# Issuing five of six early input loads from the kernel's body, after VectorE's first memset, in an attention-score kernel

## The chip, the cores and the metric

The kernel runs on one core of a Trainium2 chip. The metric is the device time of one execution in microseconds (us). The kernel before the change was run three times: 201.30, 201.58 and 201.77 us, median 201.58 us. One more execution was taken with the hardware profiler; it took 201.45 us, of which the profile covers a span of 200.1 us. All times "at" some point below are counted from the start of that span.

## The reference

For each of 8 batches and 8 heads, the scores of 512 queries against 512 keys of 64 elements are computed and scaled. There is no softmax and no mask.

```python
batch, heads, seq, dim = 8, 8, 512, 64      # q and k: float32
scale = 1.0 / np.sqrt(q.shape[-1])
return (np.einsum('bhqd,bhkd->bhqk', q, k) * scale).astype(np.float32)
```

The inputs are 8.39 MB each, 16.78 MB together. The output is 8 x 8 x 512 x 512 float32, 67.11 MB. So four fifths of all bytes moved are stores.

## The kernel before

The kernel is written with one instruction stream for each engine and explicit semaphores. SyncE issues every DMA. The input is cut into four units of two batches (`UNITS = 4`), and each unit has one load of keys and one of queries, 2.1 MB each. That makes eight loads. The output goes out in 16 stores of 4.2 MB (`ALL = 16`).

The four steps of the data are these. GpSimd casts a landed load to bf16. TensorE transposes it, and VectorE and ScalarE move the transposed tiles to `kT` and `qz`. TensorE multiplies. VectorE and ScalarE scale the scores into one of three large buffers, which SyncE then stores.

The first six loads stand inside a critical section of the tile framework. It is closed and compiled before the streams of the engines begin; at its end stands a barrier of all five engines. The last two loads reuse buffers, and wait in SyncE's stream until GpSimd has cast the third and the fourth load.

```python
    def load(v, x):
        nc.sync.dma_start(out=xf(v)[:, x],
                          in_=(k_r, q_r)[x][v].rearrange("p (s c) -> p s c", s=2)
                          ).then_inc(load_sems[2 * v + x], 16)

    with tc.tile_critical(no_gpsimd_drain=True):
        for v in range(UNITS - 1):
            for x in range(2):
                load(v, x)
    tc.close()
    tc.compile()


    for x in range(2):
        nc.sync.wait_ge(sem["ready"], 3 + x)
        load(UNITS - 1, x)
    for g in range(ALL):
        nc.sync.wait_ge(sem["act"], 4 * g + 4)
        nc.sync.wait_ge(sem["dve"], 4 * g + 4)
        nc.sync.dma_start(out=out_r[g], in_=store_buffer(g).rearrange("p x i k -> p x (i k)")
                          ).then_inc(store_sems[g % 3], 16)
    # ... (waits for the last stores)
```

GpSimd's stream: it builds the identity matrix and then casts each load in two halves as it lands.

```python
    # ... (identity)
    for v in range(UNITS):
        for x in range(2):
            # ...
            nc.gpsimd.wait_ge(load_sems[2 * v + x], 16)
            # ...
            for s in range(2):
                # ... (source and destination patterns)
                cast = nc.gpsimd.tensor_copy(out=dst, in_=src)
            cast.then_inc(sem["ready"], 1)
```

VectorE's stream begins with two memsets that clear the padded query tiles; each of them raises `zeroed` by one.

```python
    def evacuator(engine, copy, scaled, parity, done, freed):
        if parity:
            for v in range(2):
                engine.memset(qz[:, v * N:(v + 1) * N], 0.0).then_inc(sem["zeroed"], 1)
        for c in range(CHUNKS):
            engine.wait_ge(sem["turn"], c + 1)
            if c == 2:
                engine.wait_ge(sem["zeroed"], 2)
            move(copy, c, parity, first[c])
        # ... (scaling the scores, moving later chunks)
```

TensorE waits, before the first scores of output blocks 0, 1 and 2, until 2, 6 and 8 loads have been cast, since the store buffers of those blocks are also load buffers. From block 3 on it waits for the store that used the buffer before.

```python
            if p == 0 and w == 1:
                if g < 3:
                    pe.wait_ge(sem["ready"], (2, 6, 8)[g])
                else:
                    pe.wait_ge(store_sems[g % 3], g // 3 * 16)
```

Of the kernel before, what the change touches and what calls it, by code (L numbers as in the profile page):

```python
# [5 lines left out]
def kernel(  # L6
# [5 lines left out]
    nc = tc.nc  # L12
# [3 lines left out]
    UNITS = B // 2  # L16
# [21 lines left out]
    sem = {name: nc.alloc_semaphore(name) for name in names}  # L38
# [31 lines left out]
    def xf(v):  # L70
        return bigs[(0, 1, 2, 1)[v]].rearrange("p x i k -> p (x i k)").rearrange(
            "p (x s c) -> p x s c", x=2, s=2)
# [4 lines left out]
# [3 lines that stand above are left out]
                          ).then_inc(load_sems[2 * v + x], 16)  # L80

    with tc.tile_critical(no_gpsimd_drain=True):  # L82
        for v in range(UNITS - 1):
            for x in range(2):
                load(v, x)
    tc.close()
    tc.compile()  # L87


    for x in range(2):  # L90
        nc.sync.wait_ge(sem["ready"], 3 + x)
        load(UNITS - 1, x)
# [152 lines left out]
```

## Time and profile before

| quantity | value |
|---|---|
| time, median of three runs | 201.58 us |
| span of the profile | 200.1 us |
| TensorE busy with matmuls | 99.9 us, 50% |
| VectorE busy | 106.1 us, 53% |
| ScalarE busy | 84.9 us, 42% |
| GpSimd busy | 39.5 us, 20%, all of it in the first quarter |
| bytes moved by DMA | 83.95 MB, mean 419 GB/s |
| mean granted TensorE clock | 0.811 of full speed |

The profile page gives the busy time of each engine, and cuts the span into 40 slices whose digits are the busy share in tenths. The chain of waits walks back from the last instruction to what released each step. The timeline lists instructions in order of time, with the idle time ahead of them and what ended it. "SPq L78" is SyncE's queue working on line 78 of the kernel, where a load is issued. The time of such an issue is not the time of the transfer: that begins about a microsecond later and ends when the semaphore of the load has reached its full count, which the profile calls the landing.

### The profile page before, as it was taken

How to read it: one execution, taken by the hardware profiler on the slowest of the kernel's cores; microseconds unless marked ns; L12 is line 12 of the kernel's file. 1: busy time of each engine (PE TensorE's matmuls, PEld its weight loads, DVE VectorE, ACT ScalarE, POOL GpSimd, SP SyncE). 2: the span in 40 equal slices, each digit the busy share in tenths (PEclk: the TensorE clock that was granted, in tenths of full speed). 3: DMA queues.
4: the chain of work that ended last, by engine and by line, in shares of the span. 5: the costliest groups of instructions: out<-in, count | busy, mean ns of one | idle time of the engine just before them, and what ended most of it. 6: DMA issues, size and time to landing. Idle time of an engine off the chain costs nothing.

```text
span 200.1 us, 1081 instructions
## 1 busy us (share of the span) xinstructions
PE 99.9 (50%) x377; PEld 47.4 (24%) x384; DVE 106.1 (53%) x98; ACT 84.9 (42%) x97; POOL 39.5 (20%) x22
## 2 busy tenths in 40 slices
PE   0027660376875757654764487365747373830000
PEld 0026430143331414312431233041202020200000
DVE  0665692076895847691769276829364544450000
ACT  0204670264693646562665266446444343430000
POOL 0399999996000000000000000000000000000000
PEclk9999997579797888995799579969696968585555
DMA  6999999999999999999999999999999999999996
GB/s 190 439 422 429 426 442 429 422 409 426 432 436 432 422 432 432 432 429 429 432 429 432 426 439 432 432 422 439 432 429 419 426 442 429 429 419 436 429 436 259
DMA packets 5509, 83.95 MB, mean 419 GB/s; under 512 B 384, under 2 KB 384, under 8 KB 384
## 3 DMA queue, kind: packets, MB, share of 16 engines
q1 hardware_dynamic: 5504, 83.89, 98.6%
q8 instruction: 3, 0.05, 0.1%
q14 instruction: 2, 0.02, 0.0%
HBM read 16.78 MB, written 67.11 MB: 419 GB/s over the span
## 4 chain that ended last, share of the span: by engine, by line
DMA 58%; DVE 12%; PE 10%; POOL 7%; issue 1%; SPq 0%
DMA out_dram<-big 42%; DVE big L212 10%; DMA big<-in_k_dram 8%; DMA big<-in_q_dram 7%; POOL xb L122 7%; PE ps L145 7%; PE tp L130 3%; DVE qz L184 2%; DVE kT L184 1%; SPq L78 0%; SPq L95 0%; SPq L87 0%; SPq L82 0%
## 5 line engine op out<-in xcount | busy, mean ns | idle before, releaser
L145 PE MATMUL ps<-kT,qz 128*128 128x512 bf16 x249 | 79.7, 454 | 61.9 <-DMA out_dram<-big 31.1
L212 DVE TENSOR_SCALAR big<-ps 128x1024 f32<-128x1024 f32 x64 | 76.9, 1222 | 52.3 <-PE ps L145 47.9
L209 ACT ACTIVATE big<-ps 128x1024 f32<-128x1024 f32 x64 | 65.0, 1024 | 71.2 <-PE ps L145 65.9
L145 PEld LDWEIGHTS ps<-kT,qz 128*128 128x128 bf16 x256 | 25.2, 110 | 109.6 <-DMA out_dram<-big 34.4
L122 POOL CAST xb<-big 128x2048 bf16<-128x2048 f32 x16 | 38.8, 2463 | 3.7 <-DMA big<-in_k_dram 3.0
L130 PE MATMUL tp<-identity,xb 128*128 128x128 f32 x104 | 19.2, 347 | 13.7 <-POOL xb L122 13.7
L130 PEld LDWEIGHTS tp<-identity,xb 128*128 128x128 f32 x104 | 17.5, 187 | 17.6 <-issue 16.5
L184 DVE COPY kT<-tp 64x512 f32<-64x512 f32 x14 | 9.7, 694 | 6.9 <-PE tp L130 6.5
L184 ACT COPY kT<-tp 64x512 f32<-64x512 f32 x14 | 8.1, 577 | 11.5 <-PE tp L130 11.1
L189 DVE MEMSET qz<- 128x4096 uint32 x2 | 6.9, 3472 | 6.7 <-PEq L87 5.9
L184 DVE COPY qz<-tp 64x512 f32<-64x512 f32 x12 | 8.3, 695 | 3.8 <-PE tp L130 3.4
L184 ACT COPY qz<-tp 64x512 f32<-64x512 f32 x12 | 7.5, 621 | 1.7 <-PE tp L130 1.6
L130 PE MATMUL ps<-identity,xb 128*128 128x128 f32 x24 | 5.6, 420 | 1.2 <-POOL xb L122 1.2
L130 PEld LDWEIGHTS ps<-identity,xb 128*128 128x128 f32 x24 | 5.0, 226 | 1.6 <-POOL xb L122 1.6
L184 DVE COPY qz<-ps 64x512 f32<-64x512 f32 x4 | 2.8, 694 | 2.1 <-PE ps L130 2.0
L184 ACT COPY qz<-ps 64x512 f32<-64x512 f32 x4 | 2.5, 625 | 2.4 <-PE ps L130 2.4
L184 ACT ACT_TABLE_LOAD x1 | 1.3, 1283 | 5.0 <-PEq L87 5.0
L184 DVE COPY kT<-ps 64x512 f32<-64x512 f32 x2 | 1.4, 694 | 0.3 <-PE ps L130 0.3
L184 ACT COPY kT<-ps 64x512 f32<-64x512 f32 x2 | 1.2, 578 | 0.6 <-PE ps L130 0.5
L102 POOL MEMSET identity<- 128x128 f32 x1 | 0.2, 205 | 4.6 <-POOLq L87 4.6
L104 POOL TENSOR_SCALAR_AFFINE_SELECT identity<-identity 128x128 f32<-128x128 f32 x1 | 0.3, 292 | 0.2 <-POOL identity L102 0.2
L229 POOL MEMSET const-float32-0.0<- 128x1 f32 x1 | 0.1, 98 | 0.2 <-issue 0.2
(3 smaller groups left out, 0.3 us busy)
## 6 DMA issues: line engine op xcount, KB each, us to landing
out_dram<-big SPq DMA_DIRECT2D x16, 4096.0 KB, 21.3
big<-in_k_dram SPq DMA_DIRECT2D x4, 2048.0 KB, 15.6
big<-in_q_dram SPq DMA_DIRECT2D x4, 2048.0 KB, 18.0
```

The costliest lines, as they stand in the source:

```text
L102: nc.gpsimd.memset(identity, 0.0).then_inc(sem["ident"], 1)
L104: nc.gpsimd.affine_select(out=identity, in_=identity, compare_op=mybir.AluOpType.not_equal, fill=1.0, base=0, pattern=[[-1, P]], channel_m ...
L122: cast = nc.gpsimd.tensor_copy(out=dst, in_=src)
L130: ins = pe.transpose(out=dst[:, w], identity=identity, in_=xw[:, c % SLOTS * W + w])
L145: ins = pe.matmul(out=pss[pair % 3][:, w, :], lhsT=qz[:, n, i + w], rhs=keys[:, n], start=True, stop=True)
L184: copy(out=dst, in_=src[:, h]).then_inc(sem["moved"], 1)
L189: engine.memset(qz[:, v * N:(v + 1) * N], 0.0).then_inc(sem["zeroed"], 1)
L209: lambda o, ps: nc.scalar.mul(out=o, in_=ps, mul=scale),
L212: lambda o, ps: nc.vector.tensor_scalar(out=o, in0=ps, scalar1=scale, scalar2=None, op0=mult),
L229: nc = _bacc.Bacc("TRN2", target_bir_lowering=False, num_devices=1)
```

## The change

All loads but the first leave the critical section. They are issued in SyncE's own stream, after a wait for VectorE's first memset. The loads keep their order, their sizes, their buffers and their semaphores, and nothing else in the kernel is touched. The purpose is to hand the first load to the DMA engines alone, and let the other five follow when the engines have come to work.

```diff
     with tc.tile_critical(no_gpsimd_drain=True):
-        for v in range(UNITS - 1):
-            for x in range(2):
-                load(v, x)
+        load(0, 0)
     tc.close()
     tc.compile()
 
 
+    nc.sync.wait_ge(sem["zeroed"], 1)
+    for n in range(1, 2 * (UNITS - 1)):
+        load(n // 2, n % 2)
     for x in range(2):
         nc.sync.wait_ge(sem["ready"], 3 + x)
         load(UNITS - 1, x)
```

## The prediction

> **What bounds the kernel now.** I read the page first: the slices, the queues, and the chain that ended last. No compute engine is busy for more than 53% of the span; the DMA engines are.
>
> ```profile
> span 200.1 us, 1081 instructions
> DMA  6999999999999999999999999999999999999996
> GB/s 190 439 422 429 426 442 429 422 409 426 432 436 432 422 432 432 432 429 429 432 429 432 426 439 432 432 422 439 432 429 419 426 442 429 429 419 436 429 436 259
> q1 hardware_dynamic: 5504, 83.89, 98.6%
> ```
>
> The DMA row is 9 in every slice but the first and the last, at a nearly constant 430 GB/s; the one queue that SyncE feeds fills 98.6% of the 16 engines' span. 83.89 MB at 430 GB/s is 195.1 us. The other 5 us of the span are the start before data flow at full rate, and the end. So **the time is the moment at which the DMA engines begin, plus 195 us, plus every hole in their work**. That is why the first ten microseconds, the only ones the change touches, matter at all.
>
> Does the work behind the loads leave holes later? The chain of waits, in order of time, shows how the stores live:
>
> ```profile
> 62.91 19.99 DMA out_dram<-big
> ...
> 90.23 22.02 DMA out_dram<-big
> ```
>
> The columns are start, length and what it was. A store of 4.19 MB needs 9.75 us at 430 GB/s, but lands 20.0 to 22.0 us after its issue, so about 12 us of older stores stand ahead of it. A buffer returned at 62.91 + 19.99 = 82.90 is full again at 90.2, after 7.3 us. The compute side could thus be several microseconds later and the DMA engines would not notice. Conversely, making it earlier buys nothing.
>
> Now the start, in the timeline (start, length, engine, line, what; in brackets the idle time before it and what ended it):
>
> ```profile
> 0.95 0.39 SPq L78 DMA_DIRECT2D big<-in_k_dram  x1
> 1.39 0.42 SPq L78 DMA_DIRECT2D big<-in_q_dram  x1
> ...
> 3.53 0.46 SPq L78 DMA_DIRECT2D big<-in_q_dram  x1
> 5.00 0.20 POOL L102 MEMSET identity<- 128x128 f32 x1 [4.56 <-POOLq L87]
> 5.00 1.28 ACT L184 ACT_TABLE_LOAD   x1 [5.00 <-PEq L87]
> ...
> 5.93 3.47 DVE L189 MEMSET qz<- 128x4096 uint32 x1 [5.93 <-PEq L87]
> 8.71 34.24 POOL L122 CAST xb<-big 128x2048 bf16<-128x2048 f32 x14 [2.98 <-DMA big<-in_k_dram]
> ```
>
> SyncE issues six loads back to back from 0.95 to 3.99, about 0.5 us each. And **GpSimd, ScalarE and VectorE all stand idle until 5.0 us or later, released by line 87**, the end of the framework's section. What line 87 waits for is seen in the view of lines 82 and 87 (count, duration in ns, first and last start):
>
> ```profile
> L82 SPq EVENT_SEMAPHORE  x1: 17/17/17, 4.0 to 4.0; - x1
> L87 SPq DRAIN  x3: 7/7/7, 4.3 to 4.6; - x3
> L87 POOLq EVENT_SEMAPHORE  x4: 17/17/17, 4.4 to 4.9; - x4
> ```
>
> SyncE reaches the barrier only after its last issue: issues done at 3.99, its section's semaphore at 4.0, the barrier's exchanges from 4.3 to 4.9, the first work at 5.0. Every engine begins late because SyncE has issued six loads first. The chip runs that barrier 1.0 us after SyncE's last issue.
>
> Last, how fast loads go. The landing times of the key loads, then of the query loads:
>
> ```profile
> DMA to landing us min/median/max: 7.7/15.6/25.2
> DMA to landing us min/median/max: 12.2/18.0/29.6
> ```
>
> And the rates by stretch (from:to, length, busy time of the five engine rows, clock, DMA share, GB/s):
>
> ```profile
> 2.00:4.00 2.00, 0.00 (x0) 0.00 (x0) 0.00 (x0) 0.00 (x0) 0.00 (x0) 1.00 1.01 246
> 4.00:6.00 2.00, 0.00 (x0) 0.00 (x0) 0.07 (x1) 1.00 (x1) 0.50 (x2) 1.00 0.94 401
> 6.00:8.00 2.00, 0.00 (x0) 0.00 (x0) 2.00 (x1) 0.29 (x1) 0.00 (x0) 1.00 0.99 426
> ```
>
> The shortest landing of each is the first of its kind: load 0 lands at 0.95 + 7.7 = 8.65, load 1 at 1.39 + 12.2 = 13.59. One load behind another costs 4.9 us (2.10 MB at 430 GB/s); a load into an idle queue costs 7.7 us, that is 2.8 us more, for the way to the first byte, the slow first packets (246 GB/s from 2 to 4 us) and the completion.
>
> **What the Trainium skill says.** "DMA: Bandwidth & Descriptors", section "Queues, rings and completion order", says that each DMA engine consumes the descriptors of one ring in order. The trace agrees: loads issued within 3 us land 4.9 us apart, in order, so load 0 already has the engines to itself. The same page, "Anatomy of one DMA", says that DMA engines wait on no semaphore; the sequencer that issues does. So the new wait stops SyncE, and only an empty ring stops the data. That section also fits a transfer (issued from GpSimd there) as about 2.0 us plus bytes at 436 GB/s, an estimate of 6.8 us for one load; the trace shows 7.7 for the first one, and the trace is used here. The section "Specifications" gives a ceiling of 435 GB/s; at the measured 430 there is about 1% left to win.
>
> **The change part by part.**
>
> *It removes* five issues from ahead of the barrier. They ran from 1.39 to 3.99. SyncE is then done at 0.95 + 0.39 = 1.34, so the barrier and everything released by it come 3.99 - 1.34 = **2.65 us earlier**: GpSimd's and ScalarE's first work at 5.00 - 2.65 = 2.35, the first memset at 5.93 - 2.65 = 3.28.
>
> *It adds* a wait for that memset's end. Its length is 3.47 us in the timeline; it ends at 5.93 + 3.47 = 9.40 before, and at 3.28 + 3.47 = **6.75** after. A wait of SyncE on a semaphore is followed by its issue within some 0.02 us elsewhere in this trace (the cast that releases the load at 23.41 ends at 23.39). Load 1 is therefore issued at 6.77 instead of 1.39.
>
> *It moves* loads 1 to 5. Load 0 still lands at 8.65. The question is whether the rings run dry between load 0 and load 1. Bytes moved by 8.0 us, from the stretches (25, 246, 401 and 426 GB/s for 2 us each) are 2.20 MB, and load 0 is 2.10 MB, so its last bytes pass at about 7.8 on average. Load 1's first bytes come about 1.0 us after its issue, as those of load 0 did (issue 0.95, flow just before 2.0): at about 7.8. **The two meet within a few tenths of a microsecond.** Two limits bracket the cost:
> - rings never dry: load 1 lands 4.9 us after load 0, at 13.55, as before. Cost 0.
> - rings dry, with the whole start-up paid again: load 1 lands at 6.77 + 7.7 = 14.47 instead of 13.59. Cost 0.9 us.
>
> I choose 0.4: a ring that is just running empty will likely lose a part of the slow start.
>
> *What it reaches.* GpSimd casts a load in 2 x 2.45 = 4.9 us, exactly the DMA's pace, so it can't catch up: a load that lands 0.4 later is cast 0.4 later, and the last two loads, issued on the third and fourth cast (23.41 and 28.31), go out at about 23.8 and 28.7. Load 5 lands at 33.5, so the queue holds work all along. The first store, issued at 31.18 before, also has loads ahead of it. So no further hole opens, and the 0.4 arrives at the end undiminished. The 2.65 us won by VectorE, ScalarE and GpSimd are worth nothing, since the first cast waits for load 0, which lands when it did.
>
> Sum: 201.58 + 0.4 = **202.0 us**.
>
> **The rivals.**
>
> *The barrier doesn't move* (something other than SyncE's issues holds the engines to 5 us). Then load 1 goes out at 9.42, the rings are dry from 7.8, and load 1 lands at 9.42 + 7.7 = 17.1, 3.5 us late: 205.1 us, still 1.8%. For it speaks that VectorE's memset starts 0.9 us after ScalarE's first work, so a part of its delay is its own; but the second memset also starts 0.80 us after the first with nothing to wait for, so that part seems to belong to the memset, and moves along. Against it speaks the order of events at lines 82 and 87.
>
> *The first load gains from being alone* and lands sooner than 8.65, so that casting begins sooner. The slow first packets lie in the time in which SyncE issues the other five, which speaks for it; but the rings serve in order, and then GpSimd only waits for load 1. The end is set by load 1's flow, so time stays at 201.6 to 202.5.
>
> *Compute becomes the bound*, because casts and first scores shift. The 12 us of queued stores speak against it: a shift below that is hidden.
>
> *A gain*: the earlier engine start shortens the kernel. It needs a start of the data flow before 2 us, which nothing in the change moves, so at most a few tenths.
>
> **Range and chances.** The bracket is 201.6 to 202.5, the three runs spread by 0.5, and the start-up could cost a little more when GpSimd's and VectorE's work lies beside it: 201.3 to 203.0. Two per cent is 4.0 us; even the barrier rival stays inside. Chances: faster 0.01, within 2% 0.97, slower 0.02.
>
> **What would show each step.** The profile after should have the first memset at about 3.3 us, SyncE's second issue at about 6.8, load 0 landing near 8.6, load 1 at 13.5 to 14.5, later landings 4.9 us apart, a dip in the rate between 7 and 9 us, and 430 GB/s from then on. The prediction is wrong if the memset still begins at 5.9, if the rate dips for over 1 us, or if a later slice falls below 9.

## The result and the profile after

The changed kernel takes 202.45 us, the median of four runs (202.25 to 202.50), against 201.46 us for the kernel before on the same chip (201.30 to 201.77). That is 0.99 us more; the ratio is 1.0046, with a 95% interval of 1.0028 to 1.0063. So it is slower by half a per cent, a difference far below 2% but clear of noise.

The page of the changed kernel first, the same rows as were shown before:

```profile
span 201.2 us, 1081 instructions
DMA  6999999999999999999999999999999999999995
GB/s 205 345 433 420 433 443 423 420 388 437 427 430 430 433 432 425 433 433 433 420 440 423 433 430 437 430 423 440 427 433 420 433 443 423 430 427 430 433 437 254
q1 hardware_dynamic: 5504, 83.89, 98.6%
```

The DMA row still reads 9 from the second slice on, so at this resolution nothing has changed. The row below it tells where the time went: the second slice (5 to 10 us) moved 345 GB/s where it had moved 439. Over 5.03 us, 94 GB/s less is 0.47 MB, or 1.1 us at 430 GB/s. The first slice moved slightly more than before (205 against 190, worth 0.2 us). The slice that starts at 40 us moved 388 where it had moved 409; every other slice between the first two and the last lies within 12 GB/s of before.

The timeline of the start (start, length, engine, line, what; in brackets the idle time before and what ended it):

```profile
0.95 0.39 SPq L78 DMA_DIRECT2D big<-in_k_dram  x1
2.34 0.20 POOL L103 MEMSET identity<- 128x128 f32 x1 [1.90 <-POOLq L85]
2.34 1.28 ACT L185 ACT_TABLE_LOAD   x1 [2.34 <-PEq L85]
...
3.27 3.47 DVE L190 MEMSET qz<- 128x4096 uint32 x1 [3.27 <-PEq L85]
6.77 0.34 SPq L78 DMA_DIRECT2D big<-in_q_dram  x1
...
8.75 4.81 POOL L123 CAST xb<-big 128x2048 bf16<-128x2048 f32 x2 [5.68 <-DMA big<-in_k_dram]
...
14.63 9.75 POOL L123 CAST xb<-big 128x2048 bf16<-128x2048 f32 x4 [1.08 <-DMA big<-in_q_dram]
```

The engines are released 2.66 us earlier, the memset begins at 3.27 instead of 5.93, and load 1 is issued at 6.77. The first cast begins at 8.75, almost as before (8.71): load 0 landed at 8.69 against 8.66, so having the DMA engines to itself brought it nothing. The new item is the last line: GpSimd, which used to cast 14 halves without a pause, now waits 1.08 us for load 1.

The view of lines 82 and 85, the end of the critical section (count, duration in ns, first and last start):

```profile
L82 SPq EVENT_SEMAPHORE  x1: 17/17/17, 1.4 to 1.4; - x1
...
L85 POOLq EVENT_SEMAPHORE  x4: 17/17/17, 1.7 to 2.2; - x4
```

SyncE reaches the barrier at 1.4 instead of 4.0, and the barrier follows at the same distance. Then the shortest landings of the key loads and of the query loads, and below them the rates by stretch (the last figure is GB/s, the one before it the DMA share; a packet counts whole in the stretch in which it begins, so a share can exceed 1):

```profile
DMA to landing us min/median/max: 7.7/13.5/21.2
DMA to landing us min/median/max: 7.8/15.9/25.5
```

```profile
6.00:8.00 2.00, 0.00 (x0) 0.00 (x0) 1.20 (x2) 0.00 (x0) 0.00 (x0) 1.00 1.26 442
8.00:10.00 2.00, 0.00 (x0) 0.00 (x0) 2.00 (x1) 0.00 (x0) 1.25 (x1) 1.00 0.75 229
10.00:12.00 2.00, 0.00 (x0) 0.00 (x0) 1.01 (x1) 0.00 (x0) 2.00 (x2) 1.00 1.03 442
```

Load 0 takes 7.7 us and load 1 takes 7.8, from issue to landing: load 1 pays the start-up of an idle queue nearly whole, and lands at 14.58 instead of 13.55. From 8 to 10 us the rate is 229 GB/s. The later landings, read from the semaphores in the trace, are 19.48, 24.38, 29.27 and 34.16, so 4.9 us apart and each 1.02 to 1.03 us later than before. The last DMA write ends at 200.72 instead of 199.68, 1.04 us later. **A hole of 1 us at 9 us runs through to the end undiminished.**

The chain of waits shows that the stores still have a queue ahead of them:

```profile
91.41 21.89 DMA out_dram<-big
...
148.34 23.60 DMA out_dram<-big
```

At 9.75 us for one store's bytes, 22 to 24 us from issue to landing means 12 to 14 us of older stores in front. Compute never became the bound.

### The profile page after: what moved, and what is told of

The parts are those of the page before. It is cut to its first block, busy times and chain, and to the rows that moved or that the text cites. A ratio compares the mean times of both kernels' runs of the same rounds, so it can differ in the third digit from the quotient of the medians.

```text
span 201.2 us, 1081 instructions
## 1 busy us (share of the span) xinstructions
PE 98.3 (49%) x377; PEld 46.8 (23%) x384; DVE 106.1 (53%) x98; ACT 84.7 (42%) x97; POOL 39.4 (20%) x22
## 4 chain that ended last, share of the span: by engine, by line
DMA 56%; DVE 14%; PE 9%; POOL 7%; issue 1%; ACT 1%; SPq 0%
DMA out_dram<-big 42%; DVE big L213 9%; DMA big<-in_q_dram 7%; POOL xb L123 7%; DMA big<-in_k_dram 6%; PE ps L146 6%; PE tp L131 3%; DVE qz L185 2%; DVE qz L190 2%; DVE kT L185 1%; ACT big L210 1%; SPq L78 0%; SPq L96 0%
## 5 line engine op out<-in xcount | busy, mean ns | idle before, releaser
L146 PE MATMUL ps<-kT,qz 128*128 128x512 bf16 x249 | 78.1, 443 | 63.0 <-DMA out_dram<-big 32.2
L146 PEld LDWEIGHTS ps<-kT,qz 128*128 128x128 bf16 x256 | 24.6, 109 | 109.7 <-DMA out_dram<-big 35.4
```

The source lines that it names most:

```text
L146: ins = pe.matmul(out=pss[pair % 3][:, w, :], lhsT=qz[:, n, i + w], rhs=keys[:, n], start=True, stop=True)
```

## The experiments

The theory to be tested came out of the prediction: the cost is max(0, issue of load 1 + 7.8 - 13.55), that is, a queue that runs dry pays its start-up again, and a queue refilled in time pays nothing. The rivals were a fixed penalty for issuing the loads in two groups, a gain from the early start, and a barrier that has nothing to do with SyncE's issues. All experiments are edits of the changed kernel, except the one with two queues, which edits the kernel before. All were timed beside the kernel before on the same chip.

### No wait

```diff
-    nc.sync.wait_ge(sem["zeroed"], 1)
```

> Loads 1 to 5 follow the barrier with no wait at all, so SyncE issues load 1 at about 2.3 us, and the engines keep their start at 2.3 to 3.3 us. Restart theory (the cost is max(0, issue of load 1 + 7.8 - 13.55), an empty ring pays its start-up again): load 1 lands at 13.55, time as before the change, 201.5 us, ratio to before 1.000. Rival, early start helps: VectorE, ScalarE and GpSimd work 2.65 us sooner, so the time falls below before, by up to 2.6 us. Rival, fixed penalty for splitting the loads (each group of issues after a pause costs 1.0 us whatever its time): 202.4 us, ratio 1.005.

Measured: 201.50 us against 201.48, ratio 1.0000 (0.9992 to 1.0008). Load 1 is issued at 2.34 and the first memset begins at 3.27:

```profile
2.34 0.34 SPq L78 DMA_DIRECT2D big<-in_q_dram  x1
...
3.27 3.47 DVE L189 MEMSET qz<- 128x4096 uint32 x1 [3.27 <-PEq L85]
```

This run has everything of the change but the wait: the split into two groups, and engines that start 2.66 us early. Neither costs nor wins anything that the interval of 0.2 us either way would show. The fixed penalty and the gain from an early start both fall.

### The time of the second issue, shifted by the size of the memset

The memset that SyncE waits for is made shorter or longer; the second memset takes the other heads, so VectorE clears the same tiles. H is the number of heads in the first memset, 8 in the changed kernel.

```diff
-            for v in range(2):
-                engine.memset(qz[:, v * N:(v + 1) * N], 0.0).then_inc(sem["zeroed"], 1)
+            for lo, hi in ((0, H), (H, 2 * N)):
+                engine.memset(qz[:, lo:hi], 0.0).then_inc(sem["zeroed"], 1)
```

With H = 4:

> The first memset clears 4 heads (the second 12): load 1 is issued at about 5.0, about 3 us before load 0's last bytes. Restart theory: cost 0, load 1 lands at 13.55, 201.5 us, ratio 1.000. Fixed penalty: 202.4 us, ratio 1.005.

With H = 6:

> The first memset clears 6 heads instead of 8 (the second 10), so it ends about 0.87 us sooner and load 1 is issued at about 5.9. Restart theory: load 1 lands at 5.9 + 7.8 = 13.7, cost 0.1 us, 201.6 us, ratio 1.0005. Fixed penalty: 202.4 us, ratio 1.005, as in the changed kernel.

With H = 10:

> The first memset clears 10 heads (the second 6): load 1 is issued at about 7.6, 0.87 us later than in the changed kernel. Restart theory: load 1 lands at 7.6 + 7.8 = 15.4, cost 1.9 us, 203.3 us, ratio 1.009. Fixed penalty: 202.4 us, ratio 1.005.

After these three, two more between them. With H = 5:

> First memset over 5 heads (the second over 11): load 1 is issued at about 5.15 us, between the two runs at 4.62 (no cost) and 5.69 (cost 0.9 us, where the restart theory had said 0.1). If the queue has to be refilled some 3 us before its data end, and a later refill pays the start-up whole or in part, the cost here lies between 0 and 0.9 us: 201.5 to 202.4 us. A step between 5.15 and 5.69 gives 201.5, ratio 1.000; a step between 4.62 and 5.15 gives 202.4, ratio 1.0045; a slope of one gives 202.0, ratio 1.0022.

With H = 7:

> First memset over 7 heads (the second over 9): load 1 is issued at about 6.2 us, between 5.69 (cost 0.9 us) and 6.77 (cost 1.0 us in the changed kernel). If the cost is flat there, because a refill that comes too late pays one start-up whatever is left in the queue: 202.4 us, ratio 1.0045. If it rises by one with the time of issue up to the 1.0 of the changed kernel: 201.9 us, ratio 1.002.

Measured; "cost" is the difference of the medians, and "formula" is max(0, issue + 7.8 - 13.55):

| kernel | load 1 issued | load 1 landed | time, us (spread) | cost | formula |
|---|---|---|---|---|---|
| no wait | 2.34 | 13.58 | 201.50 (201.35 to 201.68) | 0.0 | 0 |
| H = 4 | 4.62 | 13.60 | 201.54 (201.32 to 201.95) | 0.1 | 0 |
| H = 5 | 5.16 | 14.26 | 202.06 (201.88 to 202.71) | 0.7 | 0 |
| H = 6 | 5.69 | 14.17 | 202.39 (201.81 to 202.73) | 0.9 | 0 |
| H = 7 | 6.22 | 14.77 | 203.06 (202.46 to 203.13) | 1.7 | 0.5 |
| H = 8, the change | 6.77 | 14.58 | 202.45 (202.25 to 202.50) | 1.0 | 1.0 |
| H = 10 | 7.83 | 15.61 | 203.39 (203.31 to 203.55) | 1.9 | 2.1 |

The ratios are 1.0003 (0.9995 to 1.0011) for H = 4, 1.0038 (1.0025 to 1.0051) for 5, 1.0042 (1.0028 to 1.0056) for 6, 1.0076 (1.0063 to 1.0088) for 7 and 1.0094 (1.0081 to 1.0107) for 10. The landings are those of each kernel's one profile, which for H = 6 and H = 7 was the fastest of its runs.

**The theory holds at both ends and fails in between.** Early enough, there is no cost; from H = 8 to H = 10, load 1 is issued 1.06 us later and lands 1.03 us later. The stretches from 8 to 10 us of H = 4 and of H = 10 show the two cases:

```profile
8.00:10.00 2.00, 0.00 (x0) 0.00 (x0) 2.00 (x1) 0.00 (x0) 1.20 (x1) 1.00 0.99 426
```

```profile
8.00:10.00 2.00, 0.00 (x0) 0.00 (x0) 1.61 (x1) 0.00 (x0) 1.29 (x1) 1.00 0.82 156
```

With H = 10 load 1 landed 2.07 us later than in the kernel before. The packets in the trace split that in two: between 7 and 10 us the 16 DMA engines stood without a packet for 1.08 us on average, and the packets that began between 5 and 11 us took, summed up for each engine, 0.98 us more than in the steady flow; together 2.06.

But "early enough" is earlier than the formula says. It puts the corner at 5.75; the runs put it between 4.62 and 5.16, which is 3.5 to 4 us before load 0 lands at 8.65. And between 5.16 and 6.22 the cost varies from run to run, and at 6.22 it is larger than at 6.77, though the intervals of the two ratios just touch. For H = 7 the query loads' landing view reads

```profile
DMA to landing us min/median/max: 8.5/16.8/26.2
```

so load 1 took 8.5 us there, longer than into an idle queue (7.7).

A reason for the odd middle is in the semaphores of the trace. A load's semaphore is raised 16 times, and the 16 times differ (us). I read them as one from each of the 16 DMA engines: their spread hardly changes from load to load (0.79 to 0.82 us for the first seven loads of the kernel before), as it would if each engine worked through a share of its own.

| load 1 done on | first engine | median engine | last engine |
|---|---|---|---|
| kernel before | 12.76 | 13.24 | 13.55 |
| H = 4 | 12.94 | 13.17 | 13.60 |
| H = 5 | 13.24 | 13.48 | 14.26 |
| H = 6 | 13.11 | 13.41 | 14.17 |
| H = 7 | 13.04 | 13.42 | 14.77 |
| H = 8, the change | 13.79 | 14.04 | 14.58 |
| H = 10 | 14.84 | 15.11 | 15.61 |

In the middle the median engine is only 0.2 us late, but the last ones are later: for H = 5 seven engines are done between 13.89 and 14.26, for H = 7 a single one at 14.77 where the next is at 13.90. In the changed kernel and for H = 10 all engines are late nearly alike. A load has landed when its last engine is done, and among the loads an engine that has fallen behind stays behind: for H = 7, load 5 is done at 32.99 on the median engine and at 34.36 on the last, still 1.4 us apart. The time of the kernel follows the last engine, though not one for one: the profiled run of H = 7, where load 1 landed 1.22 us late, took 1.1 us more than the kernel before, that of H = 6 with 0.62 took 0.3 more. Part of such a lag is lost among the stores, perhaps because one engine is 1.2 to 1.7 us behind the median there in the kernel before as well, from the second store on. That the late engines are those that found no descriptors in time fits, but what an engine waits for isn't recorded, so this stays an inference; so does the cause of the run-to-run variation, and the slower runs of H = 7, which make its median, have no profile.

### Two loads first

Load 1 goes back into the critical section, and loads 2 to 5 wait for the first memset; then the same with a wait for the second memset.

```diff
         load(0, 0)
+        load(0, 1)
...
-    for n in range(1, 2 * (UNITS - 1)):
+    for n in range(2, 2 * (UNITS - 1)):
```

```diff
-    nc.sync.wait_ge(sem["zeroed"], 1)
+    nc.sync.wait_ge(sem["zeroed"], 2)
```

With the wait for the first memset:

> Loads 0 and 1 stay in the critical section, loads 2 to 5 wait for the first memset. The barrier moves 0.45 us later than in the changed kernel, so load 2 is issued at about 7.2, while load 1 fills the rings until about 12.8. Restart theory: no dry ring, load 2 lands at 18.5 as before the change, 201.5 us, ratio 1.000. Fixed penalty for a group of issues after a pause: 202.4 us, ratio 1.005.

With the wait for the second memset:

> Loads 0 and 1 in the critical section, and the rest after the second memset instead of the first: load 2 is issued at about 11.5 us, while load 1's data end at about 12.9, so 1.4 us ahead of a dry queue, as load 1 in the changed kernel (6.77 against about 8.0). Restart theory, for any queue that runs dry at any time: load 2 lands at 11.5 + 7.8 = 19.3 instead of 18.46, cost 0.85 us, 202.3 us, ratio 1.004. Rival, the start-up belongs to the first microseconds of the kernel alone: load 2 lands at 18.5, 201.5 us, ratio 1.000.

Measured: 201.44 us against 201.45 for the first, ratio 0.9999 (0.9991 to 1.0008). Load 2 was issued at 7.23, later than load 1 in the changed kernel, and the wait was free, since load 1 still lay in the queue. With the second memset: 203.29 us against 201.39, ratio 1.0094 (1.0078 to 1.0109). From its timeline, the issue of load 2, and the cast that waits for it:

```profile
11.52 0.33 SPq L78 DMA_DIRECT2D big<-in_k_dram  x1
...
20.95 2.47 POOL L124 CAST xb<-big 128x2048 bf16<-128x2048 f32 x1 [2.36 <-DMA big<-in_k_dram]
```

The start-up is therefore no matter of the kernel's first microseconds; a queue that runs low at 12 us pays it too. But the size was a miss: 0.85 us expected, 1.9 measured. Again the last engine tells: load 2 was done at 18.81 on the median engine, 0.7 us later than before, and at 20.73 and 20.90 on the last two, over 2 us later.

### The barrier put back

Five tiny loads into an unused tile keep SyncE busy ahead of the barrier, as the five real ones did; the real ones stay behind the wait. The lines that allocate the tile and its semaphore are left out here.

```diff
         load(0, 0)
+        for n in range(5):
+            nc.sync.dma_start(out=scratch[:, n], in_=k_r[0, 0:16, 0:16]).then_inc(scratch_sem, 16)
```

> The changed kernel with five tiny loads (1 KB each, into a scratch tile nobody reads) issued after load 0 in the critical section: SyncE is as long busy ahead of the barrier as in the kernel before, while the data are those of the changed kernel. If SyncE's issues set the barrier: first memset at about 5.9, its end at 9.4, load 1 issued at 9.4 and landing at 17.2, time 201.5 + 3.65 = 205.1 us, ratio 1.018. If something else set it: memset at 3.3, 202.4 us, ratio 1.005.

Measured: 205.00 us against 201.45, ratio 1.0170 (1.0157 to 1.0184). From the timeline:

```profile
1.40 2.34 SPq L88 DMA_DIRECT2D scratch<-in_k_dram  x5
4.74 0.20 POOL L108 MEMSET identity<- 128x128 f32 x1 [4.30 <-POOLq L90]
...
5.67 3.47 DVE L195 MEMSET qz<- 128x4096 uint32 x1 [5.67 <-PEq L90]
...
9.16 0.36 SPq L81 DMA_DIRECT2D big<-in_q_dram  x1
```

SyncE's last issue ends at 3.74, and GpSimd begins 1.0 us later, as in the kernel before (3.99 and 5.00), in the changed kernel (1.34 and 2.34) and with two loads first (1.81 and 2.80). The memset, its end and load 1's issue all move back by 2.4 us, and the time grows by 2.6 us over the changed kernel. Load 1 takes 7.7 us from issue to landing, as load 0 did into an idle queue, so the tiny loads did not slow it. SyncE's issues do set the barrier. **Without the early barrier the same wait costs about 3.5 us instead of 1.0.**

### Two queues for the first load

```diff
-        for v in range(UNITS - 1):
-            for x in range(2):
-                load(v, x)
+        for s, queue in enumerate((nc.sync, nc.scalar)):
+            queue.dma_start(out=xf(0)[:, 0, s],
+                            in_=k_r[0].rearrange("p (s c) -> p s c", s=2)[:, s]
+                            ).then_inc(load_sems[0], 16)
+        for n in range(1, 2 * (UNITS - 1)):
+            load(n // 2, n % 2)
...
-            nc.gpsimd.wait_ge(load_sems[2 * v + x], 16)
+            nc.gpsimd.wait_ge(load_sems[2 * v + x], 32 if v == x == 0 else 16)
```

> The kernel before, with load 0 cut in two halves of its columns, one issued from SyncE and one from ScalarE at the same time; the other loads as before. If the slow first packets are the latency of each queue's first packet on an idle engine, two queues overlap theirs: the start-up shrinks by 0.3 to 0.8 us, 200.7 to 201.2 us, ratio 0.996 to 0.998. If the start-up is common to all packets of the first microseconds, nothing is won: ratio 1.000.

Measured: 201.43 us against 201.45, ratio 0.9998 (0.9990 to 1.0006). Nothing is won; the slow stretch is as slow as with one queue (246 GB/s before):

```profile
2.00:4.00 2.00, 0.00 (x0) 0.00 (x0) 0.00 (x0) 0.00 (x0) 0.00 (x0) 1.00 0.88 221
```

So at the kernel's start the slow first packets aren't the latency of one queue that a second one could hide. No version here beats the kernel before; the change loses by what it delays and wins nothing by what it brings forward.

## Why the prediction was right, and where it was off

The time lies inside the range, and nearly every step came as it was worked out.

- **The bound.** The DMA engines, as predicted; a hole of 1.03 us in the loads became 0.99 us of time.
- **The barrier.** 2.65 us earlier expected, 2.66 measured for GpSimd and ScalarE. The run with five tiny loads shows that SyncE's issues are the cause. The rival in which the barrier stays put (205.1 us) came out when the barrier was put back: 205.0. That it agrees to 0.1 us is partly chance, since load 1 landed 3.3 us late in that run's profile and not 3.5.
- **The issue of load 1.** 6.77 expected, 6.77 measured.
- **The early start is worth nothing.** The run without a wait had it at no cost, and gained nothing. The queue of stores that hides such shifts is 10 to 12 us by the prediction's own lines (20.0 or 22.0 less 9.75), not "about 12"; nothing rests on the difference.
- **The two ends meet.** Load 1's first packets begin at 7.75, before load 0's last have ended (8.36; the prediction had put these last bytes at about 7.8). The overlap was larger than expected, and yet it didn't save the start-up.

The step that was off is the term chosen in the sum: 0.4 us for a "ring that is just running empty". It measured 0.99, so the upper limit of the bracket (0.9) was the truth, and load 1 landed at 14.58, just above the 14.47 given as the latest. The packets in the trace show why. A packet of 16 KB takes 0.61 us in the steady flow. The packets that began between 5 and 11 us took, summed up, 0.88 us more than that for each DMA engine; in the run without a wait, 0.01 us. So load 1's packets were hardly missing (between 7 and 10 us the engines stood without one for 0.06 us on average), they were slow, as those of load 0 had been from 2 to 3.5 us (0.85 us in the changed kernel). The work of VectorE and GpSimd beside them is not the reason: in the run without a wait the second memset begins at 7.54 and the first cast at 8.74, as here, and no 16 KB packet that began between 5 and 16 us took over 0.7 us. Why the first packets after a refill are slow, the runs don't show. The prediction had taken the overlap of the two as a sign that part of the start-up would be spared, and it was not. For the same reason the sign it named for being wrong, a dip of over 1 us in the rate, did show: 164 GB/s from 8 to 9 us and 295 from 9 to 10. It stood for a cost that the range still held.

The lower limit of the bracket was wrong in its reach, too. A cost of 0 needs the refill 3.5 to 4 us before the load ahead has landed; the prediction held it possible at 1.9 (6.77 against 8.65), and the formula from 2.9 on. And the bracket's upper limit is none for a refill near the end of the load ahead: a cost of 1.7 us was measured with H = 7, and 1.9 us in the late run with two loads first, where two engines were over 2 us late.

## What to carry to other kernels

In a kernel that the DMA engines bound, a wait placed ahead of transfers costs nothing while the queue behind it is well filled. Once it isn't, the wait costs a start-up of the queue, here about 1 us, and after that every microsecond by which the queue stands empty; near the edge the cost was 0.7 to 1.7 us and varied from run to run. Here "well filled" meant the next transfer issued about 4 us before the last one landed; keeping one more 2.1 MB load in the queue made the same wait free. Look also at what the issues themselves hold up: SyncE's five issues held a barrier, and with it every engine, for 2.65 us. The time of the kernel did not depend on that until SyncE was made to wait for one of these engines.

## What the runs showed of the hardware that I had not expected

- **A DMA queue refilled while data still flow can pay the start-up whole.** In the changed kernel load 1's packets begin at 7.75, while load 0's last are under way until 8.36, and still the first 16 took 1.3 us on average instead of 0.61.
- **Among the loads, a DMA engine that falls behind does not catch up.** With H = 7 the last engine was 1.35 us behind the median at load 1, and 1.37 us at load 5.
- **A VectorE memset seems to take longer than its record.** In the changed kernel, 3.47 us is recorded for 4096 elements of a partition, and 0.80 us of idle time stands before the second memset with nothing to wait for. With other sizes that time goes with the length of the memset it precedes:

```profile
2.83 1.76 DVE L190 MEMSET qz<- 128x2048 uint32 x1 [2.83 <-PEq L85]
...
5.83 5.18 DVE L190 MEMSET qz<- 128x6144 uint32 x1 [1.23 <-issue]
```

1.23 us before 6144 elements and 0.80 before 4096 are both 0.20 ns an element, and 0.59 before 3072 (H = 10) is 0.19. I take this time to belong to the memset that follows, which no trace shows directly. Added to the recorded 0.84 or 0.85 ns it gives 1.04 ns an element. The Trainium skill, "VectorE: DVE Perf Modes", section "Zero memsets can be issued as uint32 (trn2)", states one cycle an element for a memset; at VectorE's 0.96 GHz ("Trainium Kernel Development and Optimization", section "NeuronCore Architecture") that is an estimate of 1.04 ns, and the runs agree with it if the idle time is counted in. This would also be why the memsets with H = 4, 6 and 10 ended up to 0.4 us off the times in the expectations.
